# Row dot products and softmax on one core: VectorE's code aligned to an instruction block, grouped softmaxes as wide instructions, sixteen rows summed on ScalarE, an early maximum

## The chip, the cores and the metric

The kernel runs on one core of a Trainium2 chip. The metric is the device time of one execution in microseconds (us). Most executions of one kernel agree within 0.3%, and the change studied here moves the time by about that much. Medians of several rounds are compared, against runs of the kernel before on the same chip, and the traces are read to a hundredth of a microsecond.

Two lengths appear. The **span** is what the profile covers, from the first to the last instruction of the program. The **time** is the metric; it is 1.7 us or more longer than the span.

## The reference

```python
B, N, D = 8, 4096, 512                      # x, y: float32
gram = np.matmul(x, y.transpose(0, 2, 1))
diag = np.diagonal(gram, axis1=1, axis2=2)  # only the row dot products are needed
diag = diag - diag.max(axis=-1, keepdims=True)
exp = np.exp(diag)
return exp / exp.sum(axis=-1, keepdims=True)
```

Only the diagonal is used, so the work is 8 x 4096 dot products of length 512, then a softmax over each batch of 4096. The inputs are 134.22 MB and each element is used once.

## The kernel before

Row `p*32 + r` of a batch lies in partition `p`, column block `r`. A batch is 32 "rows" of 512 elements in each of 128 partitions. There are two x buffers and one y buffer; SyncE issues every load on one queue. Below, a "fused row" is one VectorE instruction that multiplies a row of x by its row of y and adds up the products; an "all-reduce" is a GpSimd instruction that combines a value over the 128 partitions; an "instruction packet", or "fetch", is a packet that brings program code and not data.

```python
for b in range(wide):                        # wide = 6: batches 0 to 5
    load_x(b, 0, R)                          # R = 32, 8.4 MB
    load_y(b, 0, R)
    nc.scalar.activation(out=side, in_=ys[:, R - K :, :], func=Act.Copy)   # K = 6: frees y early
    dots_wide(b, 0, R - K, ys[:, : R - K, :])    # VectorE product, in place
    dots_wide(b, R - K, K, side)
    ...                                          # softmax of batches 0 to 4, on ScalarE batch by batch
    sums_wide(b)                                 # VectorE sum of 32 rows

b = B - 2                                    # batch 6
load_x(b, 0, R)
for r0 in (0, R // 2):
    load_y(b, r0, R // 2)
    for r in range(r0, r0 + R // 2):
        dot_row(b, r)                        # fused product and sum, one row

b = B - 1                                    # batch 7, loads of 16, 8, 4, 2, 1, 1 rows
for n in (16, 8, 4, 2, 1, 1):
    load_x(b, r0, n)
    load_y(b, r0, n)
    for r in range(r0, r0 + n):
        ...                                  # softmax of batches 5 and 6 in between
        dot_row(b, r)
last_softmax(b)
```

```python
def last_softmax(b):
    nc.vector.tensor_reduce(out=mxp, in_=db, axis=X, op=Alu.max)          # 32 columns
    nc.gpsimd.partition_all_reduce(out_ap=mx, in_ap=mxp, channels=P, reduce_op=bass_isa.ReduceOp.max)
    nc.vector.tensor_single_scalar(out=nmx, in_=mx, scalar=-1.0, op=Alu.mult)
    nc.scalar.activation(out=rb, in_=db, func=Act.Exp, bias=nmx, scale=1.0, accum_out=sump)
    ...
```

## Time and profile before

| | |
|---|---|
| time | 322.06 us median of 6 runs (321.82 to 322.46) |
| span of the profiled run | 320.3 us |
| VectorE busy | 247.8 us (77%) |
| input queue | 97.3% of 16 engines' span |
| last input packet ends | 314.30 us (transfer records) |

The page of the profile has the busy shares, then 40 slices of the span with the busy share in tenths, then the queues with packets, MB and their share of the time of 16 transfer engines. These are its lines that matter here.

```profile
DVE 247.8 (77%) x154; ACT 22.7 (7%) x32; POOL 3.3 (1%) x10
...
DMA  9999999999999999999999999999999999999991
...
q1 hardware_dynamic: 3888, 134.22, 97.3%
...
q14 instruction: 1, 0.01, 0.0%
```

The reader should see a kernel whose transfers are at 90% or more in every slice but the last, and one packet of instructions among them. The windows view gives the rate (columns: stretch, its length, busy time of VectorE, ScalarE and GpSimd, granted TensorE clock, share of the transfer engines' time, GB/s).

```profile
40.00:235.00 195.00, 172.89 (x16) 15.66 (x16) 0.84 (x2) 1.00 1.01 435
```

435 GB/s is what the Trainium skill ("DMA: Bandwidth & Descriptors", section "Where 436 GB/s comes from") gives as the fabric's ceiling for 16 ports; the trace agrees. Its per-core limit of about 358 GB/s on the HBM side does not show.

The timeline at the end shows the wait and the tail (start, us, engine, line, operation; in brackets idle time and what ended it).

```profile
313.58 0.69 DVE L65 SCALAR_TENSOR_TENSOR xs<-xs,ys 128x512 f32<-128x512 f32 x1
...
314.85 0.69 DVE L65 SCALAR_TENSOR_TENSOR xs<-xs,ys 128x512 f32<-128x512 f32 x1 [0.57 <-DMA ys<-in_y_dram]
...
315.58 0.19 DVE L100 TENSOR_REDUCE lmxp<-diag 128x1 f32<-128x32 f32 x1
315.87 0.37 POOL L101 PARTITION_ALL_REDUCE lmx<-lmxp  x1 [16.88 <-DVE lmxp L100]
...
316.45 0.32 ACT L103 ACTIVATE res<-diag,lnmx 128x32 f32<-128x32 f32 x1 [14.57 <-DVE lnmx L102]
```

VectorE's last row waits 0.57 us for its input, and 1.60 us pass from that row's start to the exponential.

One thing is not on the page and comes from the trace's record of single transfers. The one instruction packet (8192 bytes) starts at 276.35 us, and the data packet beside it took 1.74 us where its like took 1.21. The sixteen engines end their last input at 312.98 to 313.60 us, but for one, the one I sorted this packet to, at 314.30.

### The profile page before, as it was taken

The page shows a single profiled execution, that of the slowest core. Times are in us where ns is not written, and L with a number is a line of the kernel's source. Part 1 is how long each engine was busy: PE and PEld are TensorE (multiplying, and loading weights), DVE is VectorE, ACT ScalarE, POOL GpSimd, SP SyncE. Part 2 cuts the span into 40 slices and gives each one's busy share as a digit, 9 for nine tenths or more (in the row PEclk, how much of TensorE's full clock was granted, in tenths as well). Part 3 has the DMA queues.
Part 4 walks back from the last instruction along what each step waited for, and adds up shares of the span by engine and source line. Part 5 has one row for each costly group of instructions (what it writes and reads, how often), then busy time and mean ns, then how long its engine had stood idle before and what let it go on. Part 6 is the DMA issues. An engine that isn't in the chain of part 4 may idle for free.

```text
span 320.3 us, 310 instructions
## 1 busy us (share of the span) xinstructions
DVE 247.8 (77%) x154; ACT 22.7 (7%) x32; POOL 3.3 (1%) x10
## 2 busy tenths in 40 slices
DVE  0000079995999949999499994999959999993994
ACT  1000030000300002000200003000050100000100
POOL 0000000000000000000000000000000000000100
DMA  9999999999999999999999999999999999999991
GB/s 393 393 393 524 393 393 516 401 393 483 434 393 450 466 393 409 507 393 393 524 393 393 507 409 393 466 450 393 442 475 393 393 456 411 447 419 420 419 411 46
DMA packets 4961, 134.36 MB, mean 419 GB/s; under 512 B 1504, under 2 KB 1504, under 8 KB 2272
## 3 DMA queue, kind: packets, MB, share of 16 engines
q1 hardware_dynamic: 3888, 134.22, 97.3%
q10 hardware_dynamic: 1072, 0.13, 0.3%
q14 instruction: 1, 0.01, 0.0%
HBM read 134.22 MB, written 0.13 MB: 419 GB/s over the span
## 4 chain that ended last, share of the span: by engine, by line
DMA 60%; DVE 36%; issue 2%; SPq 0%; POOLq 0%; ACT 0%; POOL 0%; DVEq 0%; ACTq 0%
DMA ys<-in_y_dram 57%; DVE xs L58 27%; DVE xs L65 5%; DVE diag L61 4%; DMA out_dram<-res 3%; POOLq L166 0%; ACT res L94 0%; SPq L51 0%; POOL lmx L101 0%; DVE res L106 0%; DVE lmxp L100 0%; DVE lrc L105 0%; DVE bmxp L78 0%; SPq L54 0%; DVEq L58 0%
## 5 line engine op out<-in xcount | busy, mean ns | idle before, releaser
L58 DVE TENSOR_TENSOR xs<-xs,ys 128x13312 f32<-128x13312 f32 x6 | 84.2, 14025 | 62.6 <-DMA ys<-in_y_dram 62.6
L61 DVE TENSOR_REDUCE diag<-xs 128x32 f32<-128x16384 f32 x6 | 103.3, 17220 | 0.2
L65 DVE SCALAR_TENSOR_TENSOR xs<-xs,ys 128x512 f32<-128x512 f32 x64 | 39.6, 689 | 5.7 <-DMA ys<-in_y_dram 5.6
L112 ACT ACTIVATE side<-ys 128x3072 f32<-128x3072 f32 x6 | 16.6, 2763 | 185.3 <-DMA ys<-in_y_dram 185.3
L58 DVE TENSOR_TENSOR xs<-xs,side 128x3072 f32<-128x3072 f32 x6 | 20.1, 3352 | 0.0
L65 DVE DVE_READ_ACCUMULATOR xs<-xs,ys 128x1 f32 x64 | 5.4, 84 | 0.0
L80 ACT ACTIVATE bnmx<-bmx 128x2 f32<-128x2 f32 x1 | 0.2, 203 | 42.8 <-POOL bmx L79 42.8
L79 POOL PARTITION_ALL_REDUCE amx<-amxp x1 | 0.4, 386 | 231.5 <-DVE amxp L78 231.5
L80 ACT ACTIVATE anmx<-amx 128x5 f32<-128x5 f32 x1 | 0.2, 208 | 32.7 <-POOL amx L79 32.7
L94 ACT ACTIVATE res<-res,arc 128x32 f32<-128x32 f32 x5 | 1.2, 310 | 14.8 <-DVE arc L91 14.8
L82 ACT ACTIVATE res<-diag,anmx 128x32 f32<-128x32 f32 x5 | 1.5, 309 | 0.0
L79 POOL PARTITION_ALL_REDUCE bmx<-bmxp x1 | 0.7, 736 | 61.7 <-DVE bmxp L78 61.7
L103 ACT ACTIVATE res<-diag,lnmx 128x32 f32<-128x32 f32 x1 | 0.3, 321 | 14.6 <-DVE lnmx L102 14.6
L112 ACT ACT_TABLE_LOAD x1 | 1.3, 1283 | 0.7 <-PEq L155 0.7
L82 ACT ACTIVATION_READ_ACCUMULATOR res<-diag,anmx 128x1 f32 x5 | 0.9, 188 | 0.0
L105 DVE RECIPROCAL lrc<-lssum 128x1 f32<-128x1 f32 x1 | 0.2, 164 | 1.0 <-POOL lssum L104 1.0
L86 POOL PARTITION_ALL_REDUCE bssum<-bsump x1 | 0.8, 797 | 1.1 <-ACT res L82 1.1
L94 ACT ACTIVATE res<-res,brc 128x32 f32<-128x32 f32 x2 | 0.5, 312 | 3.2 <-DVE brc L91 3.2
L82 ACT ACTIVATE res<-diag,bnmx 128x32 f32<-128x32 f32 x2 | 0.6, 314 | 0.0
L101 POOL PARTITION_ALL_REDUCE lmx<-lmxp x1 | 0.4, 367 | 16.9 <-DVE lmxp L100 16.9
L102 DVE TENSOR_SCALAR lnmx<-lmx 128x1 f32<-128x1 f32 x1 | 0.2, 153 | 0.5 <-POOL lmx L101 0.5
L86 POOL PARTITION_ALL_REDUCE assum<-asump x1 | 0.5, 459 | 2.0 <-ACT res L82 2.0
(13 smaller groups left out, 2.7 us busy)
## 6 DMA issues: line engine op xcount, KB each, us to landing
ys<-in_y_dram SPq DMA_DIRECT2D x3, 4096.0 KB, 15.0
xs<-in_x_dram SPq DMA_DIRECT2D x1, 4096.0 KB, 14.7
xs<-in_x_dram SPq DMA_DIRECT2D x1, 2048.0 KB, 19.2
ys<-in_y_dram SPq DMA_DIRECT2D x1, 2048.0 KB, 19.6
xs<-in_x_dram SPq DMA_DIRECT2D x1, 1024.0 KB, 8.0
ys<-in_y_dram SPq DMA_DIRECT2D x1, 1024.0 KB, 10.2
xs<-in_x_dram SPq DMA_DIRECT2D x1, 512.0 KB, 11.0
ys<-in_y_dram SPq DMA_DIRECT2D x1, 512.0 KB, 11.7
```

The source lines that it names most:

```text
L58: nc.vector.tensor_tensor(out=xt, in0=xt, in1=yt, op=Alu.mult)
L61: nc.vector.tensor_reduce(out=diag[:, b, :], in_=xs[b % 2], axis=X, op=Alu.add)
L65: nc.vector.scalar_tensor_tensor(out=xt[:, r, :], in0=xt[:, r, :], scalar=1.0, in1=ys[:, r, :], op0=Alu.mult, op1=Alu.mult, accum_out=diag ...
L79: nc.gpsimd.partition_all_reduce(out_ap=mx, in_ap=mxp, channels=P, reduce_op=bass_isa.ReduceOp.max)
L80: nc.scalar.mul(nmx, mx, -1.0)
L82: nc.scalar.activation(out=res[:, b0 + i, :], in_=diag[:, b0 + i, :], func=Act.Exp, bias=nmx[:, i : i + 1], scale=1.0, accum_out=sump[:, i ...
L86: nc.gpsimd.partition_all_reduce(out_ap=ssum, in_ap=sump, channels=P, reduce_op=bass_isa.ReduceOp.add)
L94: nc.scalar.activation(out=rb, in_=rb, func=Act.Copy, scale=rc[:, i : i + 1])
L101: nc.gpsimd.partition_all_reduce(out_ap=mx, in_ap=mxp, channels=P, reduce_op=bass_isa.ReduceOp.max)
L102: nc.vector.tensor_single_scalar(out=nmx, in_=mx, scalar=-1.0, op=Alu.mult)
L103: nc.scalar.activation(out=rb, in_=db, func=Act.Exp, bias=nmx, scale=1.0, accum_out=sump)
L112: nc.scalar.activation(out=side, in_=ys[:, R - K :, :], func=Act.Copy)
```

## The change

The intent: let VectorE's code lie within one block of instructions, so that no instruction packet disturbs a transfer engine near the end, and shorten the tail. There are four parts.

- VectorE's code starts at a multiple of 128 instructions, and 32 of the 64 fused rows become wide products (16 of them with wide sums, 16 with sums on ScalarE), which makes VectorE's code shorter.
- The softmaxes of batches 0 to 4 and of 5 and 6 are done by wide instructions, mostly on VectorE.
- The first 16 rows of batch 7 are multiplied by VectorE in two wide products and summed row by row on ScalarE.
- The maximum over 30 of the last batch's 32 columns is taken before the last two rows arrive.

```diff
+    nc.vector.addr_align(128, offset=0, max_nops=0)
-    for b in range(wide):
+    for b in range(whole):                       # 5: batches 0 to 4
 ...
+    first.largest()                              # max of batches 0 to 4, all-reduce on GpSimd
+    b = whole                                    # batch 5, y in two halves
+    load_x(b, 0, R)
+    load_y(b, 0, H)
+    products(b, 0, H)
+    first.exps()                                 # one wide subtraction, one wide Exp
+    load_y(b, H, H)
+    products(b, H, H)
+    first.total()
+    sums(b, 0, R)
+    first.store(2)                               # the store of five batches in two transfers
+    b += 1                                       # batch 6
+    load_x(b, 0, R)
+    load_y(b, 0, H)
+    products(b, 0, H)                            # instead of 16 fused rows
+    sums(b, 0, H)
+    load_y(b, H, H)
+    dots(b, H, H)                                # 16 fused rows, as before
+    second.largest()
+    b += 1                                       # batch 7
 ...                                              # its first loads, 16 rows of x and of y
+    products(b, 0, H // 2)
+    second.exps()
+    sums_act(b, 0, H // 2)                       # ScalarE, row by row
+    products(b, H // 2, H // 2)
+    second.total()
+    sums_act(b, H // 2, H // 2)
 ...                                              # then loads of 8, 4, 2, 1, 1 rows, fused rows
+        if r0 == R - 2:
+            nc.vector.tensor_reduce(out=last[:, R:], in_=last[:, :r0], axis=X, op=Alu.max)
```

```diff
 def last_softmax(b):
-    nc.vector.tensor_reduce(out=mxp, in_=db, axis=X, op=Alu.max)
-    nc.gpsimd.partition_all_reduce(out_ap=mx, in_ap=mxp, ...)
-    nc.vector.tensor_single_scalar(out=nmx, in_=mx, scalar=-1.0, op=Alu.mult)
+    nc.gpsimd.partition_all_reduce(out_ap=mx, in_ap=last[:, R - 2 :], ...)   # 3 columns
+    nc.vector.tensor_reduce(out=nmx, in_=mx, axis=X, op=Alu.max, negate=True)
```

More of the change, by code (lines that the diff above doesn't have):

```diff
@@ L27 @@
     R = N // P
-    wide = B - 2
+    H = R // 2
+    K = 6
+    whole = B - 3
     xv = x.rearrange("b (p r) d -> b p r d", p=P)
@@ L40 @@
     ys = big.tile([P, R, D], f32, name="ys")
-    K = 6
     side = big.tile([P, K, D], f32, name="side")
-    diag = small.tile([P, B, R], f32, name="diag")
+    diag = small.tile([P, B - 1, R], f32, name="diag")
+    last = small.tile([P, R + 1], f32, name="last")
     res = small.tile([P, B, R], f32, name="res")
@@ L48, in column, with dot_column, rows @@
         return small.tile([P, n], f32, name=name)
+    def dot_column(b, r0, n):
+        return last[:, r0 : r0 + n] if b == B - 1 else diag[:, b, r0 : r0 + n]
+    def rows(b, r0, n):
+        return xs[b % 2][:, r0 : r0 + n, :]
     def load_x(b, r0, n):
-        nc.sync.dma_start(out=xs[b % 2][:, r0 : r0 + n, :], in_=xv[b, :, r0 : r0 + n, :])
+        nc.sync.dma_start(out=rows(b, r0, n), in_=xv[b, :, r0 : r0 + n, :])
     def load_y(b, r0, n):
         nc.sync.dma_start(out=ys[:, r0 : r0 + n, :], in_=yv[b, :, r0 : r0 + n, :])
-    def dots_wide(b, r0, n, yt):
-        xt = xs[b % 2][:, r0 : r0 + n, :]
-        nc.vector.tensor_tensor(out=xt, in0=xt, in1=yt, op=Alu.mult)
@@ L60, in sums_wide @@
-    def sums_wide(b):
-        nc.vector.tensor_reduce(out=diag[:, b, :], in_=xs[b % 2], axis=X, op=Alu.add)
-    def dot_row(b, r):
-        xt = xs[b % 2]
-        nc.vector.scalar_tensor_tensor(
-            out=xt[:, r, :],
-            in0=xt[:, r, :],
-            scalar=1.0,
-            in1=ys[:, r, :],
-            op0=Alu.mult,
-            op1=Alu.mult,
-            accum_out=diag[:, b, r : r + 1],
-        )
-    def group_exp(name, b0, n):
-        mxp, mx, nmx, sump, ssum = (column(name + s, n) for s in ("mxp", "mx", "nmx", "sump", "ssum"))
-        nc.vector.tensor_reduce(out=mxp, in_=diag[:, b0 : b0 + n, :], axis=X, op=Alu.max)
-        nc.gpsimd.partition_all_reduce(out_ap=mx, in_ap=mxp, channels=P, reduce_op=bass_isa.ReduceOp.max)
-        nc.scalar.mul(nmx, mx, -1.0)
-        for i in range(n):
-            nc.scalar.activation(
-                out=res[:, b0 + i, :], in_=diag[:, b0 + i, :], func=Act.Exp,
-                bias=nmx[:, i : i + 1], scale=1.0, accum_out=sump[:, i : i + 1],
-            )
-        nc.gpsimd.partition_all_reduce(out_ap=ssum, in_ap=sump, channels=P, reduce_op=bass_isa.ReduceOp.add)
-        return ssum
@@ L89, in group_out, with products @@
-    def group_out(name, b0, n, ssum):
-        rc = column(name + "rc", n)
-        nc.vector.reciprocal(out=rc, in_=ssum)
-        for i in range(n):
-            rb = res[:, b0 + i, :]
-            nc.scalar.activation(out=rb, in_=rb, func=Act.Copy, scale=rc[:, i : i + 1])
-        nc.scalar.dma_start(out=ov[:, b0 : b0 + n, :], in_=res[:, b0 : b0 + n, :])
-    def last_softmax(b):
-        db, rb = diag[:, b, :], res[:, b, :]
-        mxp, mx, nmx, sump, ssum, rc = (column("l" + s, 1) for s in ("mxp", "mx", "nmx", "sump", "ssum", "rc"))
-        nc.vector.tensor_reduce(out=mxp, in_=db, axis=X, op=Alu.max)
-        nc.gpsimd.partition_all_reduce(out_ap=mx, in_ap=mxp, channels=P, reduce_op=bass_isa.ReduceOp.max)
-        nc.vector.tensor_single_scalar(out=nmx, in_=mx, scalar=-1.0, op=Alu.mult)
+    def products(b, r0, n, yt=None):
+        xt = rows(b, r0, n)
+        nc.vector.tensor_tensor(out=xt, in0=xt, in1=ys[:, r0 : r0 + n, :] if yt is None else yt, op=Alu.mult)
@@ new lines, in sums, with sums_act, dots @@
+    def sums(b, r0, n):
+        nc.vector.tensor_reduce(out=dot_column(b, r0, n), in_=rows(b, r0, n), axis=X, op=Alu.add)
+    def sums_act(b, r0, n):
+        for r in range(r0, r0 + n):
+            row = xs[b % 2][:, r, :]
+            nc.scalar.activation(out=row, in_=row, func=Act.Copy, accum_out=dot_column(b, r, 1))
+    def dots(b, r0, n):
+        for r in range(r0, r0 + n):
+            xt = xs[b % 2][:, r, :]
+            nc.vector.scalar_tensor_tensor(
+                out=xt, in0=xt, scalar=1.0, in1=ys[:, r, :], op0=Alu.mult, op1=Alu.mult,
+                accum_out=dot_column(b, r, 1),
+            )
@@ new lines, with __init__, wide, largest @@
+    class Group:
+        def __init__(self, name, b0, n):
+            self.b0, self.n = b0, n
+            self.mxp, self.mx, self.sump, self.ssum, self.rc = (
+                column(name + s, n) for s in ("mxp", "mx", "sump", "ssum", "rc")
+            )
+            self.d, self.e = diag[:, b0 : b0 + n, :], res[:, b0 : b0 + n, :]
+        def wide(self, t):
+            return t.unsqueeze(2).to_broadcast([P, self.n, R])
+        def largest(self):
+            nc.vector.tensor_reduce(out=self.mxp, in_=self.d, axis=X, op=Alu.max)
+            nc.gpsimd.partition_all_reduce(
+                out_ap=self.mx, in_ap=self.mxp, channels=P, reduce_op=bass_isa.ReduceOp.max
+            )
+        def exps(self):
+            nc.vector.tensor_tensor(out=self.e, in0=self.d, in1=self.wide(self.mx), op=Alu.subtract)
+            nc.scalar.activation(out=self.e, in_=self.e, func=Act.Exp)
+        def total(self):
+            nc.vector.tensor_reduce(out=self.sump, in_=self.e, axis=X, op=Alu.add)
+            nc.gpsimd.partition_all_reduce(
+                out_ap=self.ssum, in_ap=self.sump, channels=P, reduce_op=bass_isa.ReduceOp.add
+            )
+        def store(self, *cuts):
+            nc.vector.reciprocal(out=self.rc, in_=self.ssum)
+            nc.vector.tensor_tensor(out=self.e, in0=self.e, in1=self.wide(self.rc), op=Alu.mult)
+            for i, j in zip((0, *cuts), (*cuts, self.n)):
+                i, j = self.b0 + i, self.b0 + j
+                nc.scalar.dma_start(out=ov[:, i:j, :], in_=res[:, i:j, :])
@@ L103, in last_softmax @@
+    def last_softmax(b):
+        db, rb = last[:, :R], res[:, b, :]
+        mx = column("lmx", 3)
+        nmx, sump, ssum, rc = (column("l" + s, 1) for s in ("nmx", "sump", "ssum", "rc"))
+        nc.gpsimd.partition_all_reduce(
+            out_ap=mx, in_ap=last[:, R - 2 :], channels=P, reduce_op=bass_isa.ReduceOp.max
+        )
+        nc.vector.tensor_reduce(out=nmx, in_=mx, axis=X, op=Alu.max, negate=True)
         nc.scalar.activation(out=rb, in_=db, func=Act.Exp, bias=nmx, scale=1.0, accum_out=sump)
@@ L112 @@
         nc.scalar.activation(out=side, in_=ys[:, R - K :, :], func=Act.Copy)
-        dots_wide(b, 0, R - K, ys[:, : R - K, :])
-        dots_wide(b, R - K, K, side)
-        if b == wide - 1:
-            group_out("a", 0, wide - 1, first)
-        sums_wide(b)
-        if b == wide - 2:
-            first = group_exp("a", 0, wide - 1)
-    b = B - 2
-    load_x(b, 0, R)
-    for r0 in (0, R // 2):
-        load_y(b, r0, R // 2)
-        for r in range(r0, r0 + R // 2):
-            dot_row(b, r)
-    b = B - 1
-    r0 = 0
-    for n in (16, 8, 4, 2, 1, 1):
+        products(b, 0, R - K)
+        products(b, R - K, K, side)
+        sums(b, 0, R)
+    first = Group("a", 0, whole)
+    first.largest()
+    b = whole
+    load_x(b, 0, R)
+    load_y(b, 0, H)
[4 more added lines that the diff above has]
+    first.total()
+    sums(b, 0, R)
+    first.store(2)
[6 more added lines that the diff above has]
+    dots(b, H, H)
+    second = Group("b", whole, 2)
+    second.largest()
+    b += 1
+    load_x(b, 0, H)
+    load_y(b, 0, H)
+    products(b, 0, H // 2)
[4 more added lines that the diff above has]
+    sums_act(b, H // 2, H // 2)
+    r0 = H
+    for n in (8, 4, 2, 1, 1):
         load_x(b, r0, n)
         load_y(b, r0, n)
-        for r in range(r0, r0 + n):
-            if r == 2:
-                second = group_exp("b", B - 3, 2)
-            if r == 10:
-                group_out("b", B - 3, 2, second)
-            dot_row(b, r)
+        if r0 == H:
+            second.store()
+        if r0 == R - 2:
+            nc.vector.tensor_reduce(out=last[:, R:], in_=last[:, :r0], axis=X, op=Alu.max)
+        dots(b, r0, n)
         r0 += n
```

## The prediction

> **What bounds the kernel.** Data transfer. The DMA row of the 40 slices is at 9 tenths until the last slice, and the queue table gives the input queue 97.3% of 16 engines' span for 134.22 MB. From 40 to 235 us the windows view shows 435 GB/s. In the trace's transfer records 64 KB packets take 2.418 us on each of 16 engines; all inputs at their packet durations take about 311.4 us. The records start at 1.7 us, and the last input packet ends at 314.30. VectorE is busy 77%, but each load's wait is on work that ends 4 to 5 us before the queue would run dry, so making VectorE faster buys nothing there. I expect the body of the kernel not to move. What can move is the 6 us after the transfers, and how evenly the engines finish.
>
> **Uneven finish.** Sorted into 16 engines by their packets, fifteen end their input between 312.98 and 313.60 us, one at 314.30. That one carried the single instruction fetch of the span (an 8192-byte packet at 276.35, 0.31 us), and its data packet beside it took 1.74 us where its like take 1.21: about 0.84 us lost. VectorE's last row waited 0.57 us for this. The Trainium skill ("Runtime: NRT & Kernel Launch", section "Instruction fetch mechanics") says instructions are refilled in blocks by a DMA queue of the sequencer's own; the trace agrees, though its packet is 8 KB, half the block it names. The change aligns VectorE's code and shortens it (32 fused rows with their accumulator reads instead of 64), so it should cross no block boundary: no fetch, and the last input lands near 313.6, 0.7 us earlier.
>
> **The tail.** Row 31 ends at 315.55; a 32-column maximum (0.19), the GpSimd all-reduce (0.37) and a negation (0.15) follow, exp starts at 316.45. After: the all-reduce takes three columns directly, and one 3-column maximum with negation (about 0.19) stands for the negation. That removes about 0.25 us. The rest (exp, sum, reciprocal, product, store) is unchanged.
>
> **VectorE in the last batches** (estimated from 1.04 ns per column for products, 1.05 for sums, 0.61 us a fused row). Batch 6's first half becomes slower (17.3 us against 9.8), batch 7's first half faster (8.8 us for two products against 9.8, its sums on ScalarE at about 0.7 us a row, done near 310.4). Chained from 231.8 us, VectorE ends row 29 near 313.6, the early maximum near 313.75, row 31 near 315.0. So it, not the landing, probably ends last, and eats some 0.3 us of the 0.7. Loads stay ahead: batch 6's and 7's are issued 4 us or more before they are needed. The store of five batches cut in two clears its first part sooner and the wait of a later load with it (13.7 us of waiting for a store on the DMA queue before), but the queue never ran dry, so that gains nothing.
>
> Sum: about 0.4 us (landing, as far as VectorE lets it) + 0.25 us (maximum) = 0.65 us.
>
> **Predicted: 321.3 us, range 320.7 to 322.0.** Faster by over 2%: 0.01; within 2%: 0.98; slower by over 2%: 0.01.
>
> **What would show it.** Right: no instruction packet within the span, an input queue still near 97%, last input landing at 313.5 to 313.8, from row 31's end to exp about 0.65 us instead of 0.9, span near 319.5. Wrong: a fetch still in the span (then about 321.8), or an idle DMA slice near 290 to 312 us.
>
> **What would make it wrong.** VectorE later than chained (each microsecond after 315.5 is a microsecond lost); ScalarE's sums not done at 313.6, holding the early maximum; a load held by the semaphore of a small store, starving the queue; alignment adding a fetch at the start that delays one engine.

## More of the kernel before

The chain of waits, in order of time (start, us, what), is this around the fifth y and at the end of the kernel before.

```profile
172.28 24.51 DMA ys<-in_y_dram
196.79 0.03 issue
196.82 0.02 DVEq L58
196.84 0.04 issue
196.89 14.04 DVE xs L58
...
210.98 24.62 DMA ys<-in_y_dram
...
280.06 14.66 DMA ys<-in_y_dram
...
310.12 4.64 DMA ys<-in_y_dram
314.76 0.03 issue
314.79 0.02 DVEq L65
314.81 0.04 issue
314.85 0.71 DVE xs L65 x2
```

Every stage shown here ends with VectorE waiting for a y.

## The result, and the profile after

| | before | after |
|---|---|---|
| time, median of 6 runs | 322.06 us (321.82 to 322.46) | 323.06 us (322.32 to 323.22) |
| span of the profiled run | 320.3 us | 320.3 us |
| time minus span, profiled run | 1.8 us | 2.1 us |
| VectorE busy | 247.8 us | 255.5 us |
| instruction packet among the loads | at 276.3 us | at 4.8 us |
| last input packet ends | 314.30 us | 314.53 us |
| row 31 ends (accumulator read) | 315.55 us | 315.82 us |

The ratio is 1.0024 (95% interval 1.001 to 1.0037). Ratios here are the mean time of one kernel's fast runs over that of the other's of the same rounds, so not quite the ratio of the medians quoted. The interval excludes 1: the changed kernel is a little slower, and it was forecast to be a little faster (321.3 us). Its six runs have two lengths: two have a span of 320.3 us and four of 321.0 to 321.1. The profiled run is one of the two short ones.

The page of the changed kernel, the lines that answer to those above:

```profile
DVE 255.5 (80%) x100; ACT 25.9 (8%) x42; POOL 15.0 (5%) x10
...
DMA  9999999999999999999999999999999899999992
...
q1 hardware_dynamic: 4032, 134.22, 97.4%
...
q14 instruction: 1, 0.01, 0.0%
```

There is still one instruction packet. In the transfer records it starts at 4.8 us (another, at 322.1 us, is after the span). The data packet that starts as it ends, at 5.13 us, took 2.95 us where its like take 2.42: with the packet's own 0.31 that is about 0.84 us lost on one engine, as in the kernel before.

What brings it can be seen as well. The view of the alignment's line shows that it is a branch of VectorE (operation, count, duration in ns, first and last start in us); the kernel before has none.

```profile
L135 DVEq COMPARE_BRANCH  x1: 47/47/47, 0.7 to 0.7; - x1
```

The packet follows this branch by 4.1 us. The windows view of the changed kernel:

```profile
40.00:235.00 195.00, 175.38 (x17) 13.81 (x5) 2.39 (x1) 1.00 1.00 431
```

The chain of waits of the changed kernel from the fifth y on:

```profile
172.99 24.52 DMA ys<-in_y_dram
197.51 0.03 issue
197.54 0.02 DVEq L66
197.56 0.04 issue
197.61 17.31 DVE xs L66 x2
214.91 0.02 issue
214.94 17.23 DVE diag L69
...
232.61 8.75 POOL amx L99
...
285.44 9.81 DVE xs L79 x32
...
295.58 4.48 POOL bmx L99
...
315.13 0.71 DVE xs L79 x3
```

There are two things to see. The fifth y ends its step at 197.51 us instead of 196.79, 0.72 later. And after it no transfer appears in the chain any more: from 197.6 to 315.8 us VectorE, with a few waits for GpSimd, leads to the end of this profiled run. In the kernel before, transfers stand at 210.98, 280.06 and 310.12. The timeline at the end:

```profile
314.41 0.18 DVE L184 TENSOR_REDUCE last<-last 128x1 f32<-128x30 f32 x1
314.51 0.69 DVE L79 SCALAR_TENSOR_TENSOR xs<-xs,ys 128x512 f32<-128x512 f32 x1
...
315.13 0.69 DVE L79 SCALAR_TENSOR_TENSOR xs<-xs,ys 128x512 f32<-128x512 f32 x1
...
315.92 0.37 POOL L124 PARTITION_ALL_REDUCE lmx<-last  x1 [10.65 <-DVE xs L79]
...
316.57 0.32 ACT L128 ACTIVATE res<-last,lnmx 128x32 f32<-128x32 f32 x1 [6.17 <-DVE lnmx L127]
```

Row 31 no longer waits for its load. The early maximum works: 1.44 us from that row's start to the exponential instead of 1.60.

**How a lagging transfer engine is seen.** Each load ends with sixteen 4-byte packets in the records, which I read as one for each transfer engine. For a large load, the time from the first to the last of them (the "spread") is then how far the slowest engine is behind the fastest. A load has landed only when the slowest is done. This table, made from the records, is the base of what follows ("y0" is the first batch's y, "x5" the sixth's x; the values are of each kernel's profiled run).

```
profiled run      instruction      first    y0 complete,   x5 complete,   last input
                  packets (us)     load     spread         spread         ends
before            276.3            1.71     41.58  0.57    215.84  0.65   314.30
after             4.8              1.72     41.95  0.93    216.82  1.33   314.53
control           5.2              1.72     42.29  1.23    217.79  1.94   315.47
no_align          289.2            1.73     41.50  0.49    216.39  1.24   315.08
before_align      5.1, 309.3       1.73     42.18  1.16    217.32  1.71   315.30
act_b6            4.8, 287.9       1.72     41.90  0.93    216.78  1.33   315.12
early_align       1.2              1.92     41.81  0.60    216.54  0.67   314.30
before_early      1.2, 300.4       1.92     41.75  0.63    216.06  0.55   314.68
act_b6_early      1.2, 1.3         1.95     41.68  0.53    216.05  0.40   314.02
two_aligns        5.0, 63.8        1.72     42.08  1.11    218.38  2.24   316.04
before_offset_116 123.6, 310.2     1.73     41.70  0.70    217.75  2.11   315.65
```

The same records show what one packet does, in any of the profiled runs. Eleven instruction packets fall between 60 and 305 us. The data packet that starts as one of them ends takes 0.28 to 0.66 us longer than its like, and across nine of the eleven the spread rises by 0.37 to 0.95 us from the load before to one of the next two (no_align: from 1.16 to 2.11 across the packet at 289.2). Across the other two it does not rise (act_b6 at 287.9, vector_only at 287.0).

They also show delays that no instruction packet explains. Among the data packets that start between 195 and 200 us, those of four profiled runs took 8.3 to 15.0 us more in sum than the median of their size (control 9.5, with two packets of over 4 us; before_align 8.9; two_aligns 15.0; before_offset_116 8.3). In the other sixteen it is at most 2.5 (after: 0.7). These four are the only profiled runs with a span over 321.1 us. All four also have an instruction packet between 4.7 and 124 us, as among the others only after and act_b6 have. So an early packet goes with these slow packets in four profiled runs of six, and none of the fourteen without one has them; how the one would lead to the other is not shown. This stretch was chosen after the records had been seen.

### The profile page after: what moved, and what is told of

The parts are those of the page before. It is cut to its first block, busy times and chain, and to the rows that moved or that the text cites. A ratio compares the mean times of both kernels' runs of the same rounds, so it can differ in the third digit from the quotient of the medians.

```text
span 320.3 us, 270 instructions
## 1 busy us (share of the span) xinstructions
DVE 255.5 (80%) x100; ACT 25.9 (8%) x42; POOL 15.0 (5%) x10
## 4 chain that ended last, share of the span: by engine, by line
DVE 50%; DMA 44%; POOL 4%; issue 1%; SPq 0%; POOLq 0%; DVEq 0%
DMA ys<-in_y_dram 44%; DVE xs L66 30%; DVE diag L69 13%; DVE xs L79 6%; POOL amx L99 3%; POOL bmx L99 1%; DVE res L104 0%; POOLq L213 0%; POOL bssum L109 0%; SPq L59 0%; POOL lmx L124 0%; DVE amxp L98 0%; DVE res L131 0%; DVE asump L108 0%; DVE bmxp L98 0%
## 5 line engine op out<-in xcount | busy, mean ns | idle before, releaser
L66 DVE TENSOR_TENSOR xs<-xs,ys 128x13312 f32<-128x13312 f32 (+2 forms) x10 | 105.0, 10501 | 59.4 <-DMA ys<-in_y_dram 59.4
L69 DVE TENSOR_REDUCE diag<-xs 128x32 f32<-128x16384 f32 (+1 forms) x7 | 112.0, 15999 | 0.2
L140 ACT ACTIVATE side<-ys 128x3072 f32<-128x3072 f32 x5 | 13.8, 2763 | 184.5 <-DMA ys<-in_y_dram 184.5
L79 DVE SCALAR_TENSOR_TENSOR xs<-xs,ys 128x512 f32<-128x512 f32 x32 | 19.8, 688 | 0.0
L99 POOL PARTITION_ALL_REDUCE amx<-amxp x1 | 8.7, 8737 | 232.2 <-DVE amxp L98 232.2
L66 DVE TENSOR_TENSOR xs<-xs,side 128x3072 f32<-128x3072 f32 x5 | 16.8, 3352 | 0.0
L74 ACT ACTIVATE xs<-xs 128x512 f32<-128x512 f32 x16 | 9.8, 613 | 0.0
L99 POOL PARTITION_ALL_REDUCE bmx<-bmxp x1 | 4.5, 4469 | 44.5 <-DVE bmxp L98 44.5
L74 ACT ACTIVATION_READ_ACCUMULATOR xs<-xs 128x1 f32 x16 | 3.0, 186 | 0.0
L79 DVE DVE_READ_ACCUMULATOR xs<-xs,ys 128x1 f32 x32 | 2.7, 84 | 0.0
```

The source lines that it names most:

```text
L66: nc.vector.tensor_tensor(out=xt, in0=xt, in1=ys[:, r0 : r0 + n, :] if yt is None else yt, op=Alu.mult)
L69: nc.vector.tensor_reduce(out=dot_column(b, r0, n), in_=rows(b, r0, n), axis=X, op=Alu.add)
L74: nc.scalar.activation(out=row, in_=row, func=Act.Copy, accum_out=dot_column(b, r, 1))
L79: nc.vector.scalar_tensor_tensor(out=xt, in0=xt, scalar=1.0, in1=ys[:, r, :], op0=Alu.mult, op1=Alu.mult, accum_out=dot_column(b, r, 1),)
L99: nc.gpsimd.partition_all_reduce(out_ap=self.mx, in_ap=self.mxp, channels=P, reduce_op=bass_isa.ReduceOp.max)
```

## The experiments

**Theory A.** The alignment did not remove the fetch, it moved it. VectorE branches to a new block at once, and the packet comes at about 5 us, among the first loads. It holds one transfer engine up, that engine stays behind, so every load lands late, and VectorE, which the change left without slack from the fifth y on, hands the delay to the end.
**Rival B.** The added VectorE work alone is the cause (255.5 us busy against 247.8).
**Rival C.** Aligned code costs time by itself, by padding or outside the span.

### control: the changed kernel again

No edit.

> The changed kernel again, unaltered. In its first six runs it had two spans, 320.3 us (time 322.3) and 321.1 us (time 323.1); if that is chance from run to run both show again within these rounds, if it is a matter of the chip or of the loading then only one shows. Any theory: the one instruction packet near 5 us, VectorE busy without a pause of a microsecond from the landing of the fifth y to row 31.

Measured: 322.93 us (322.45 to 323.38), ratio 1.0025 (1.0012 to 1.0038). Both lengths appeared within these rounds on one chip: spans of 320.4 to 320.6 in three runs, 321.1 to 321.3 in three. So they vary from run to run. The profiled run is a long one; in it row 31 did wait, 0.33 us, for a last input that ended at 315.47, so that VectorE alone leads to the end holds only for the short kind.

```profile
315.95 0.69 DVE L79 SCALAR_TENSOR_TENSOR xs<-xs,ys 128x512 f32<-128x512 f32 x1 [0.33 <-DMA ys<-in_y_dram]
```

What chooses between the two stays open. The slow data packets near 196 us are a lead: 9.5 us in this long run and 0.7 in the short one make, over 16 engines, a difference of about 0.55 us (an estimate), where the two lengths differ by 0.7. But only one run of each length was profiled; and the kernel before had a run with a span of 321.2 us too, one of the eleven of these rounds.

### no_align: the alignment taken out

```diff
-    nc.vector.addr_align(128, offset=0, max_nops=0)
```

> The changed kernel without the address alignment. Theory A (the alignment only moves the fetch: near 5 us it delays one transfer engine, so every y lands late by 0.5 to 0.7 us, and VectorE, which has no slack from the fifth y on, hands this to the end): the fetch comes after 270 us, the first y lands near 41.9 instead of 42.4, the fifth near 196.8 instead of 197.5, span 0.4 to 0.8 us below the control, time near 321.6. Rival B (the added 9 us of VectorE work alone makes it late; the fetch does nothing): landings and span as the control within 0.2 us.

Measured: 322.44 us (322.15 to 322.86), ratio 1.0011 (0.9999 to 1.0023), on the control's chip. The fetch came at 289.2 us, the first y's wait in the chain ended at 41.86 and VectorE started at 41.95, as the theory had it, where in the control it started at 42.86. On the fifth y it started at 197.14 (196.8 was expected), in the control at 197.89. The median is 0.49 us under the control's; the intervals of the two ratios overlap. The time itself was forecast at 321.6 and is 0.8 us above that: the profiled run's last input ended at 315.08, probably since the fetch at 289 held up an engine near the end (the spread rose from 1.16 to 2.11 us across it). Rival B as the only cause falls, since the landings moved without any change of VectorE's work.

### before_align: the alignment alone

```diff
+    nc.vector.addr_align(128, offset=0, max_nops=0)
     for b in range(wide):
         load_x(b, 0, R)
```

> The kernel before with the alignment alone. Theory A: the y landings are late by 0.5 us or more from the first on, but VectorE has 4 to 5 us of slack in batches 5 and 7, so the lateness does not reach the end; a second fetch near 305 us; span within 0.5 us of the kernel before, ratio 1.000 to 1.002. Rival C (the alignment costs time by itself, outside the span, in padding or a fetch at the program's end): time minus span grows from 1.7 to 2.0 us, ratio 1.001 at an unchanged span.

Measured: 323.41 us (323.02 to 323.90), ratio 1.0042 (1.0029 to 1.0054). The one line costs 1.35 us, more than either theory said. The packets came at 5.1 and 309.3 us. Time minus span stayed at 1.8 us, so rival C's "outside the span" falls. My part of theory A that VectorE's slack would hide the delay is wrong too: row 31 waited for a last input that ended at 315.30. In this kernel the lateness was still there at the last load, and slack of VectorE does not help there. One engine's 0.84 us alone does not make 1.35: this profiled run also has 8.9 us of slow data packets near 196 us.

### act_b6: VectorE given slack

```diff
     products(b, 0, H)                            # batch 6
-    sums(b, 0, H)
+    sums_act(b, 0, H)                            # 16 rows on ScalarE
```

> The changed kernel with the sums of batch 6's first 16 rows on ScalarE, row by row, instead of one VectorE reduction of 8.7 us. Theory A and B: VectorE then waits for landings again, ends before the last one, and the end is bound by the transfers: row 31 starts right after the last landing, span 0.1 to 0.7 us below the control. If the span stays as the control's, VectorE's lack of slack is not what ends it.

Measured: 322.80 us (322.71 to 323.01), ratio 1.0022 (1.001 to 1.0034). The end is bound by the last landing (row 31 waited 0.39 us), but the median is only 0.13 us under the control's. ScalarE's code is longer now, and a second instruction packet came at 287.9 us. With the fetch at 5 us in place, slack buys nothing that can be told from the scatter. The run changes two things, the slack and ScalarE's packet, and does not part them.

### early_align: the same alignment, ahead of the loads

The alignment is put at the head of VectorE's program, ahead of the barrier that starts all engines.

```diff
-    nc.vector.addr_align(128, offset=0, max_nops=0)   # start of the kernel's body
+    nc.vector.addr_align(128, offset=0, max_nops=0)   # first instruction of VectorE's program
```

> The changed kernel with the same alignment of VectorE's code, but placed at the head of VectorE's program, ahead of the barrier that starts all engines, some 8 us before the first load. Theory A (the alignment moved the fetch to 5 us, among the loads): the fetch now comes before the first load and none is in the span, the first y lands at 41.9 instead of 42.4 to 42.9, the fifth at 196.8 to 197.2, span 319.4 to 320.2, ratio to before 0.997 to 1.000 where the control had 1.0025. Rival C (aligned code is slower by itself, or the changed kernel's other parts cost the time): ratio stays at 1.001 to 1.003.

Measured: 322.29 us (322.18 to 322.57), ratio 1.0007 (0.9994 to 1.0019). The packet came at 1.2 us: within the span, against the letter of my expectation, but before the first data packet. The first load was issued at 0.93 us instead of 0.72, and its first packet started at 1.92 instead of 1.72. The spread at the first y is 0.60, as in the kernel before, instead of 0.93 and 1.23. The body's instructions are the same; the moment of the branch and of the fetch differs, and perhaps also where in its block the body lies. The ratio's expected range was missed by 0.0007, and its interval reaches into the ranges of both theories, so this run alone does not decide. In the profiled run, the longest of its five, the end is still bound by VectorE, which ran from the fifth y to row 31 (315.20) without a wait for a transfer in the chain. Its start on the fifth y was not earlier than the changed kernel's 197.61, where 196.8 to 197.2 was expected:

```profile
197.67 17.30 DVE xs L66 x2
```

So the gain is shown by the times of the rounds and by the spread, and not by this y.

### before_early: the same for the kernel before

> The kernel before with the alignment at the head of VectorE's program. Its VectorE code is longer than one block of 128 instructions, so the fetch in the span comes once, later than before: near 307 us in place of 276. Theory A: without the fetch at 5 us the 1.35 us that the alignment alone cost are gone; y landings as in the kernel before, ratio 0.999 to 1.002. Rival C: ratio stays near 1.004.

Measured: 322.28 us (322.13 to 323.01), ratio 1.0009 (0.9997 to 1.0022). The 1.35 us of before_align shrank to 0.2 by moving the same line ahead of the barrier. The later fetch came at 300.4, not 307. The intervals of these two ratios are apart. So it matters when the branch and its fetch come, and rival C falls. How theory A's one late engine makes the whole 1.35 us is not shown.

### two_aligns: the suspected cost doubled

```diff
         sums(b, 0, R)
+        if b == 0:
+            nc.vector.addr_align(128, offset=0, max_nops=0)
```

> The suspected cost doubled: the changed kernel with a second alignment after the first batch's sums, so that VectorE enters a second new block at about 77 us. Theory A: two instruction packets in the span, near 5 and near 82 us; if they fall on two engines the later landings are about as late as with one, if on one engine another 0.8 us; so ratio 1.0025 to 1.006 and never under the control's by more than 0.001. If the fetch costs nothing: 1.0025 as the control.

Measured: 323.58 us (323.30 to 324.16), ratio 1.0048 (1.0036 to 1.0061). The page's line of the instruction queue now has two packets:

```profile
q14 instruction: 2, 0.02, 0.0%
```

They came at 5.0 and 63.8 us. I had expected the second at 82; but the branch stands in the trace at 59.98 us, when the first batch's sums (59.96 to 77.18) had just started.

```profile
L145 DVEq COMPARE_BRANCH  x1: 47/47/47, 60.0 to 60.0; - x1
```

Across the second packet the spread rose from 1.12 to 1.88 us, and later to 2.24 at x5, where this run has its 15.0 us of slow data packets near 196 us. Taken out, kept, doubled: ratios 1.0011, 1.0025, 1.0048.

### act_b6_early: both at once

VectorE given slack as in act_b6; both VectorE's and ScalarE's code aligned at the heads of their programs.

> The sums of batch 6's first 16 rows on ScalarE (VectorE then has slack before the end), with VectorE's and ScalarE's code both aligned at the heads of their programs, so that neither should fetch within the span. Theory A: no instruction packet in the span, the end bound by the last landing near 313.6 to 314.1, span 319.3 to 319.9, ratio 0.996 to 0.999: faster than both kernels. If the ratio stays at 1.002 as with act_b6, neither the fetch nor VectorE's slack is what costs.

Measured: 321.85 us (321.73 to 321.89), ratio 0.999 (0.9977 to 1.0004); span 319.7. No instruction packet fell among the loads. The timeline of its end:

```profile
314.51 0.69 DVE L79 SCALAR_TENSOR_TENSOR xs<-xs,ys 128x512 f32<-128x512 f32 x1 [0.40 <-DMA ys<-in_y_dram]
...
315.96 0.32 ACT L128 ACTIVATE res<-last,lnmx 128x32 f32<-128x32 f32 x1 [6.86 <-DVE lnmx L127]
```

Row 31 waits for its load again, and the exponential starts at 315.96 instead of 316.45 (before) and 316.57 (changed). The median is 0.2 us under the kernel before of the same rounds, but the interval includes 1, so "faster than both kernels" is shown only against the changed one. Against early_align of the same rounds, whose end VectorE bound, it is 0.44 us less: with no packet among the loads in either, that is what VectorE's slack is worth (all five runs of the one lie below all five of the other). The profiled span is 0.6 us under before's, and the median time only 0.2: time minus span is 2.15 us here.

### best_again, one_store, late_max, vector_only

This set takes act_b6_early as its control ("the best version") and undoes one part each.

> The best version so far (batch 6's first sums on ScalarE, both codes aligned at the program's head) once more, as the control of this set: ratio 0.998 to 1.000, span 319.5 to 319.8, time minus span 2.15 us.

Measured: 321.83 us (321.64 to 322.31), ratio 0.999 (0.9978 to 1.0003), time minus span 2.13 to 2.21. The profiled run was the slowest, with a span of 320.1.

```diff
-    first.store(2)
+    first.store()
```

> The best version with the first five batches stored by one transfer, not two. If the 0.25 us that all descendants of the changed kernel spend outside the span (time minus span 2.0 to 2.2 us where before has 1.75) come from the one transfer more at the program's end, time minus span falls to 1.9 or below and the time by 0.2 us; otherwise both stay as in the control of this set.

Measured: 321.78 us (321.78 to 322.17), ratio 0.999 (0.9977 to 1.0002), time minus span 2.14 to 2.18. The second store is not the cause of the time outside the span, and cutting the store in two gains nothing that shows.

```diff
-        if r0 == R - 2:
-            nc.vector.tensor_reduce(out=last[:, R:], in_=last[:, :r0], axis=X, op=Alu.max)
 def last_softmax(b):
+    nc.vector.tensor_reduce(out=mxp, in_=db, axis=X, op=Alu.max)   # and all-reduce, negation as before
```

> The best version without the early maximum: after the last row a 32-column maximum, an all-reduce of one column, a negation, as in the kernel before. The traces say that the early maximum shortens the way from row 31's start to the exponential from 1.60 to 1.45 us; in a kernel whose end is bound by the last landing all of that should show: 1.60 us in the trace and 0.1 to 0.2 us more time than the control of this set. My prediction's term was 0.25.

Measured: 322.33 us (322.02 to 322.70), ratio 1.0004 (0.999 to 1.0018), 0.50 us over best_again; in the trace 1.73 us from row 31's start (314.56) to the exponential (316.29), against 1.45. So the early maximum is worth 0.28 us by the trace (1.60 us had been expected there). The rest of the 0.5 is not explained; the intervals of the two ratios overlap.

vector_only leaves ScalarE's code where it was:

> The best version with VectorE's code aligned early and ScalarE's not: ScalarE's fetch comes back near 288 us. Theory A: one transfer engine falls about 0.7 us behind in the last 25 us, as in the kernel before, and the end is bound by it: last landing 0.2 to 0.7 us later than in the control of this set, time 0.2 to 0.7 us more. If a fetch does not matter: no difference.

Measured: 322.31 us (322.02 to 322.62), ratio 1.0002 (0.9989 to 1.0014), 0.48 us over best_again. ScalarE's packet came at 287.0. The profiled runs do not show the forecast later landing (last input 314.44 against 314.38), since best_again's profiled run was its slowest. So the times agree with theory A, though the intervals of the two ratios overlap, and the traces of this pair do not show how.

### offset_24 and before_offset_72, and four more placements

Of the miss, the time outside the span was still open: 1.7 to 1.8 us in all forms of the kernel before, about 2.0 to 2.2 in those of the changed one (except for one run of early_align, 2.53, and for two_aligns, whose second alignment moves the later code: 1.72 to 2.10).

```diff
-    nc.vector.addr_align(128, offset=0, max_nops=0)    # act_b6_early
+    nc.vector.addr_align(128, offset=24, max_nops=0)
```

> The best version with VectorE's code starting 24 instructions past a block boundary instead of at it, so that its last 20 or so instructions, after row 29, lie in the next block. Theory D (the time outside the span depends on how near to the end of its block VectorE's code ends: 15 to 48 instructions into a block gave 1.75 us, 89 to 122 gave 2.05, 127 gave 2.2, by my count): time minus span falls from 2.2 to 1.75, span stays at 319.5 to 319.8 with its new fetch after the last landing, time 321.3 to 321.5. Rival E (it depends on something else in the changed kernel): 2.2 stays.

Measured: 321.74 us (321.28 to 322.17), ratio 0.9988 (0.9974 to 1.0001). Time minus span is 1.74 to 1.80 us in all five runs, against 2.13 to 2.21 in best_again. But the spans were longer and more scattered (319.5 to 320.4), so the time gained 0.1 us at most. A new packet came at 314.04 us; the last input of that run ended at 314.61.

> The kernel before with VectorE's code aligned at the program's head and starting 72 instructions past a block boundary, so that by my count it ends some 120 instructions into a block. Theory D: time minus span rises from 1.75 to about 2.05. Rival E: 1.75 stays. The fetch in the span comes near 275 us as in the kernel before.

Measured: 321.99 us (321.74 to 322.06), ratio 0.9997 (0.9983 to 1.0011), time minus span 1.74 to 1.81. Theory D's rise did not come. The fetch came at 270.0, not 275, so my count of instructions was not right and the code may not have ended where I meant. Four placements were to cover the block, one look each (state unknown, since each ran once).

> One of four placements (24, 48, 96, 116 instructions past a block boundary) of the kernel before's VectorE code; 0 and 72 gave a time minus span of 1.75 us. Theory D: somewhere among the four VectorE's code ends late in a block, and there time minus span is 2.0 to 2.2 us. Rival E (only the changed kernel's code can show it): 1.75 in all four.

> Second of the four placements. Theory D: 2.0 to 2.2 us outside the span in at least one of the four; rival E: 1.75 in all four.

> Third of the four placements. Theory D: 2.0 to 2.2 us outside the span in at least one of the four; rival E: 1.75 in all four.

> Fourth of the four placements. Theory D: 2.0 to 2.2 us outside the span in at least one of the four; rival E: 1.75 in all four.

| label | time | time minus span | instruction packets at |
|---|---|---|---|
| before_offset_24 | 322.36 | 1.8 | 1.3 and 298.5 us |
| before_offset_48 | 322.82 | 1.8 | 1.3 and 281.8 us |
| before_offset_96 | 321.85 | 1.8 | 268.7 and 314.6 us |
| before_offset_116 | 323.42 | 1.8 | 123.6 and 310.2 us |

At none of the six placements tried does the kernel before show 2.0 us outside its span. So the placement was seen to move those 0.4 us in the changed form only, and what else is needed stays open. Nor does every branch bring a packet among the loads: with the offsets 72, 96 and 116 the branch at 0.1 us is there and no packet follows near 1.2 us. The last line is one run with a time as long as before_align's. Its packet at 123.6 us goes with a rise of the spread from 0.70 to 1.07 us only; the rest, to 2.11 at x5, came with the slow data packets near 196 us.

## Why the prediction was wrong, point by point

- **What bounds the kernel** was right: the queue is at 97.3 to 97.5% in the pages of the kernel before, the changed one and act_b6_early, and no version moved by more than 0.5%.
- **"So it should cross no block boundary: no fetch, and the last input lands near 313.6"** is the step that failed. There was a fetch, at 4.8 and 5.2 us in the two profiled runs. The last input ended at 314.53 and 315.47. The simplest reading is that branching to an aligned place is itself the entry into a new block, and that its packet comes some 4 us later, among the loads. The branch is in the trace (0.75 us), every variant with the alignment in the kernel's body has a packet 4.0 to 4.4 us after it, at 4.8 to 5.2 us, and none of the others has. I had named this as the last of the things that could make me wrong and gave it no weight; and the time that I gave for a fetch still in the span, 321.8 us, was too low as well, by 0.6 us for the short runs and 1.3 for the median. Taking the line out gained 0.5 us, adding it to the kernel before cost 1.35 us, a second one cost 0.65 us more (323.58 against 322.93, on different chips), and moving it ahead of the loads took 1.15 us of the 1.35 away in the kernel before and 0.7 of the changed kernel's 0.9 (medians against before of the same rounds).
- **An early packet went with a larger loss than its own 0.84 us.** The term "0.84 us lost" was right for one engine, in the kernel before and for the early packets too, but I booked it as a loss at the end only. After an early fetch the spread of the engines is 0.93 to 1.23 us at the first y where it is 0.49 to 0.70 in the table's other runs (up to 0.81 in runs outside the table), and it is no smaller 170 us later. The spread at x5 scatters (1.24 in no_align, 1.47 in offset_24, neither with a packet among the loads before it), and the largest values there came with the slow data packets near 196 us. So some delay has other causes, which stay open.
- **VectorE's chain** was right in its length: forecast from 231.8 to about 315.0 us, measured from 232.43 to 315.82, so 83.2 against 83.4 us. Its start was wrong by about the 0.6 us by which it was late after the fifth y. That start is not the fetch's alone: early_align's profiled run, without the early fetch, had it too (232.49). That VectorE would end last was right for the short run that was profiled. In the long one (control) the last landing did.
- **The tail's 0.25 us** was 0.16 against the kernel before (1.60 to 1.44 us), and 0.28 when undone in late_max. It was not lost, only hidden.
- **Time outside the span** was not in the prediction at all. It costs the changed kernel 0.25 us. The runs show that it changed with the placement of VectorE's code in this form (from 2.2 to 1.77 us with 24 instructions' offset) and not with the number of stores. They do not show the mechanism.

The sum for the short run of the profile: row 31 ended 0.8 us later than forecast, the way to the exponential was 0.1 longer than forecast (0.75 against 0.65), and 0.25 lay outside the span. Together that is about 1.1 us, which is the difference between 322.36 and 321.3. The median, 323.06, is that of the longer kind; the two lengths of the changed kernel's runs, 0.7 us apart, remain unexplained but for the lead named under control.

One thing I had not costed is visible in the groups of the changed kernel (count, then busy us and mean ns, then idle time before): GpSimd's all-reduces.

```profile
L99 POOL PARTITION_ALL_REDUCE amx<-amxp x1 | 8.7, 8737 | 232.2 <-DVE amxp L98 232.2
L99 POOL PARTITION_ALL_REDUCE bmx<-bmxp x1 | 4.5, 4469 | 44.5 <-DVE bmxp L98 44.5
L109 POOL PARTITION_ALL_REDUCE assum<-asump x1 | 0.5, 453 | 9.3 <-DVE asump L108 9.3
```

In the kernel before the first of them took 0.39 us, in a gap of VectorE:

```profile
L79 POOL PARTITION_ALL_REDUCE amx<-amxp x1 | 0.4, 386 | 231.5 <-DVE amxp L78 231.5
```

Under a VectorE product with two inputs, of 8.68 us, it took 8.74, under one of 4.42 us 4.47, and under a one-input sum of 17.2 us 0.45. This agrees with the Trainium skill ("SBUF — State Buffer", section "Who interferes with whom"): an instruction of VectorE with two SBUF inputs contends with a GpSimd instruction that reads SBUF, a reduction does not. In control, where the all-reduce of bmx started at 295.87 us, ahead of the product (295.94), it took 0.37 us. The long all-reduces cost the chain only two waits of 0.27 and 0.26 us, since the products stand there anyway.

## What to carry to other kernels

Where transfers run without a pause, a single instruction packet on one transfer engine is a cost like any other (here 0.6 to 1.0 us of that engine), and an early one can last to the end, because a load is done only when its slowest engine is. Before code is aligned to avoid a fetch, ask when the branch to the aligned place makes its own fetch, and put it ahead of the loads. And ask what work added to an engine does to its slack: here, in the short runs' profile, 8 us more of VectorE work turned a late fifth y into a late end. And profile a kernel's long run and its short run before one mechanism is given the whole difference.

## What the Trainium skill lacked or had wrong

- "Runtime: NRT & Kernel Launch", section "Instruction fetch mechanics", gives refills in 16 KiB blocks. All instruction packets among these runs' loads are of 8192 bytes.
- The same section calls the cost of crossing a block boundary mostly hidden. For the data it is not hidden here: in no_align the spread of the transfer engines rose from 1.16 to 2.11 us across the packet at 289.2 us. The page does not say that a packet of instructions delays data on its engine (in the kernel before, 1.74 us behind it for a packet that takes 1.21).
- "DMA: Bandwidth & Descriptors", section "Where 436 GB/s comes from", says that the HBM side (about 358 GB/s) binds transfers between HBM and SBUF, beside a measurement of its own of 425. This core, used alone, read at 435 GB/s for 195 us.
- No page has that time outside the profiled span depends on where an engine's code lies: 2.13 to 2.21 us at a block boundary, 1.74 to 1.80 with an offset of 24 instructions, otherwise the same kernel.
